# An encoder block on one core: the order of ScalarE and VectorE in its first stage, and of its last products

## The chip, the cores and the metric

One core of a Trainium2 chip runs the whole program once. The core has five engines with a queue of instructions each: TensorE (PE in the profile, PEld for its weight loads), VectorE (DVE), ScalarE (ACT), GpSimd (POOL) and SyncE (SP), which here only issues DMAs. An engine works through its queue in order; where an instruction needs another engine's result or a transfer, it waits on a semaphore, and everything behind it on its engine waits too. The metric is the device time of one execution in microseconds.

## What is computed

One layer of an encoder on 1024 tokens of 1024 channels, all in float32. Cut to what matters here:

```python
h = h + 0.5 * swiglu(rms_norm(h, ffn1_norm), w_gate, w_up, w_down)     # first stage
u = rms_norm(h, mix_norm); z = u @ w_in
h = h + (g_attn * attention(z) + g_ssm * s5(z)) @ w_out
h = h + 0.5 * swiglu(rms_norm(h, ffn2_norm), w_gate2, w_up2, w_down2)
h = h + (p @ w_ple) * sigmoid(rms_norm(h, ple_norm) @ w_ple_gate)
return rms_norm(h, final_norm)                                        # last stage

def rms_norm(x, g): return x * rsqrt(mean(x * x) + 1e-6) * g
def swiglu(x, wg, wu, wd): return (silu(x @ wg) * (x @ wu)) @ wd
```

The change touches how the first `rms_norm` and the first products of the first `swiglu` are started, and the end of the last `rms_norm`.

## The kernel before

Everything is held transposed: channels on the 128 partitions in eight tiles `h[j]`, tokens along the free axis in two halves, t=0 (columns 0 to 511) and t=1. A tile `h[j][t]` is 128x512. A matmul is done in three TensorE products (`mm3`, L190): each float32 operand is split into a rounded part and a remainder by `split` (L159): ScalarE writes the rounded part (`ph`, `xh`, `wh`; L160), VectorE subtracts it (`pl`, `xl`, `wl`; L161).

The first stage has three pieces of work.

- *The p products.* `p @ w_ple` is done at once, in the loop over n = 0..15 at the end of the quoted part: six products into a PSUM bank `pp`, a ScalarE copy out of it, and a DMA of 256 KB on GpSimd's queue. The table `hooks` says what else is written down ahead of the n-th step.
- *The norm of x.* `Norm.add` squares a tile (ScalarE) and adds it to `acc` (VectorE); `Norm.stat` sums over partitions with a matmul with `ones` into a bank `ms`, then `rstd` forms `rs`, with one ScalarE activation and three VectorE instructions. `Seven.norm` scales a tile in place (L337) and `Seven.put` splits it. `s7.nn[0]` is the norm of t=0 (`x0`), `s7.nn[1]` that of t=1 (`x1`). The four operands are named a11 and a12 (t=0, tiles 0-3 and 4-7) and a21 and a22 (t=1).
- *The FFN's first products.* `Ffn.run` first does eight C steps (11, 12, 22, 21; gate `g` and up `u` each), 24 products a step, with the first pair of column blocks of `w_gate` and `w_up`. Then come the A steps, which use seven products in place of eight and therefore need sums of operands (`sums`: s1, s3, s2, s4) and of weight blocks (`b_operand`); the operands of a step are written ahead of need by `prep`, and `need` and `prep` force the generator on.

Order: SyncE's loads stand in program order. Generators (`s7_first`, `sums`, `gen_all`) are moved on by `tick()`, once after each `mm3`, so that a `yield 14` is a distance in products. TensorE's instructions stand as written. VectorE's and ScalarE's are put in order by a scheduler, except between `order_cm.__enter__()` and `order_cm.__exit__()`, where they keep the order in which they are written among themselves; what is written outside may be put in between. In the kernel before this part ends with the p loop. The pairs of column blocks are numbered from 0 (the C steps); `begun` is called before the A steps of pair 2 (`("A", 2, 0, 0)`). GpSimd squares and sums four tiles of x1 in `x1_first`.

The last stage, `end`, finishes the last 256-column parts: `products(6, 2)` and `products(7, 2)` are 24 products each, `fin[1].stat` is the final norm's statistic of the columns 512 to 767, set by `after(7, ...)` seven `mm3` into them; `finish` scales two tiles at a time and stores them. There VectorE and ScalarE keep the written order too.

Of the kernel before, what the change touches and what calls it, by code (L numbers as in the profile page):

```python
# [20 lines left out]
NK = 8  # L21
# [20 lines left out]
def encoder_block(ctx, tc, I, out):  # L42
# [274 lines left out]
    class Seven:  # L317
# [3 lines left out]
        def __init__(self, h, gi, new_hi=None):  # L321
            self.h, self.gi = h, gi
            self.ops = {name: [] for name in ("a21",) + A7}
            self.last = []
            self.new_hi = new_hi or tw
            self.blk = [[at("hid", [P, HT], F32, "wblk") for _ in range(4)] for _ in range(2)]
            self.lo = [tx("wl") for _ in range(4)]
            self.nn = [Norm(h, t, thid("acc", dt=F32), thid("rs", dt=F32)) for t in range(2)]
            self.a21 = [(tx("xh"), tx("xl")) for _ in range(4)]
# [15 lines left out]
        def first(self, wait, then, every):  # L345
            yield wait
            self.nn[0].stat(self.nn[0].rs, self.nn[0].a0 is not self.nn[0].acc)
            yield then
            for name, j0 in (("a11", 0), ("a12", 4)):
                for k in range(4):  # L350
                    self.norm(j0 + k, 0)
                    self.put(name, self.h[j0 + k][0])
                    yield every

        def second(self, wait, every):
            yield wait
            self.nn[1].stat(self.nn[1].rs)
            yield 1
            for name, j0 in (("a21", 0), ("a22", 4)):
                for k in range(4):  # L360
                    self.norm(j0 + k, 1)
                    self.put(name, self.h[j0 + k][1])
                    yield 1

# [24 lines left out]
    class Ffn:  # L389
# [33 lines left out]
        def sums(self, every):  # L423
# [4 lines left out]
            def each(name, op, src):  # L428

                for k in range(4):  # L430
                    with behind_():
                        op(k)
                    S.put(name, src(k))
                    yield every
# [125 lines left out]
        def run_c(self, c, g):  # L560
            o = bank("gu"[g] + c)
            for half, (a, n) in enumerate((("a" + c[0] + "1", int(c[1]) - 1), ("a" + c[0] + "2", int(c[1]) + 1))):
                self.need(a)
                hi, lo = self.made["C", g, n]
                for k in range(4):
                    mm3(o, (hi[:, ksl(k)], lo[:, ksl(k)]), self.ops[a][k], half == 0 and k == 0, half == 1 and k == 3)
                    tick()
            with tc.high_priority(offset=PRI):
                self.evac_c(c, g, o)
# [385 lines left out]
    def begun():  # L955

        up_cm.__exit__(None, None, None)
        pools["gp"] = tc.tile_pool(name="gp", bufs=1)
# [4 lines left out]
    def p_split(x):  # L963
        split(*x[0], x[1])

    x0, x1 = s7.nn
    for k in range(2):
# [3 lines left out]

    def x1_first(j):
        if j == 0:
            x1.acc = x1.a0
            G.tensor_tensor(x1.acc, h[0][1], h[0][1], ALU.mult)
            return
        sq = tmp("sq")
        G.tensor_tensor(sq, h[j][1], h[j][1], ALU.mult)
        G.tensor_tensor(x1.acc, x1.acc, sq, ALU.add)

    def s7_first():
        yield from s7.first(14, 2, 2)
        for j in range(4, NK):
            x1.add(j)
        yield from chain(s7.second(6, 1), ffn.sums(2), gen_all())

# [5 lines left out]
             6: lambda: (p_split(pl_[0, 1]), p_split(pl_[1, 1])),  # L992
             9: lambda: x1_first(0), 10: lambda: x1_first(1), 11: lambda: x1_first(2), 12: lambda: x1_first(3),
             13: lambda: ffn.prep(("C", "11", 0))}
    start(s7_first())
    for n in range(2 * NK):
# [9 lines left out]
        nc.gpsimd.dma_start(pp_d[m, t], pp)  # L1006
    order_cm.__exit__(None, None, None)
    ffn.run()
# [826 lines left out]
    def end():  # L1835

        start(after(7, fin[1].stat))
        six = products(6, 2)
        drain()
        finish(1, (0,))  # L1840
        A.activation(six[2], six[0], AF.Sigmoid)
        added(*six)
        a, b, s, hm = products(7, 2)
        A.activation(s, a, AF.Sigmoid)
        fin[2].square(6, A)
        finish(1, (2,))
# [116 lines left out]
```

## Time and profile before

| | us |
|---|---|
| runs before (three) | 2104.4, 2106.75, 2111.21; median 2106.75 |
| profiled execution | 2106.68 |
| its span | 2104.9 |
| TensorE busy | 2040.9 (97%) |
| VectorE busy | 1495.0 (71%) |
| ScalarE busy | 1015.5 (48%) |
| GpSimd busy | 496.3 (24%) |
| mean granted clock of TensorE | 0.987 |

The profiled execution's time is the span and what lies around it (1.8 us). Busy time is a sum of instructions, and TensorE's are pipelined: a product lasts 0.39 us and the next starts 0.23 us later, so its 97% says that it nearly always has work, not that the work is done at its best rate. The page's slices show where it has none; the reader should look at the first and the last of them.

### The profile page before, as it was taken

What the parts mean: (1) busy time and instruction counts of PE and PEld (TensorE: products, weight loads), DVE (VectorE), ACT (ScalarE), POOL (GpSimd) and SP (SyncE); (2) the same over time, 40 slices, a digit from 0 to 9 for tenths busy, and PEclk for the clock granted to TensorE, in tenths of its full rate; (3) what the DMA queues carried; (4) which work ended last, traced back from release to release, by engine and by line L of the source; (5) the groups of instructions that cost most, each with busy time, mean ns of one, the idle gap of its engine ahead of it and who ended that gap; (6) DMA issues with size and microseconds to landing.
All of it is one profiled execution on the core that took longest, in us unless ns stands there. A gap on an engine that the chain in (4) does not pass through costs nothing.

```text
span 2104.9 us, 28181 instructions
## 1 busy us (share of the span) xinstructions
PE 2040.9 (97%) x9378; PEld 1687.5 (80%) x9378; DVE 1495.0 (71%) x2551; ACT 1015.5 (48%) x1908; POOL 496.3 (24%) x723
## 2 busy tenths in 40 slices
PE   5999999999999999999998999999999999999997
PEld 4788888888888887788887788788888888888886
DVE  5878787676696774788864668896656555796765
ACT  4533333334444443577766556553333333444554
POOL 2005565553000052888823002000000000000000
PEclk8899999999999999999999999999999999999999
DMA  6234344439443356787767688133332337443332
GB/s 221 95 118 132 124 135 128 139 119 327 153 153 113 120 143 172 235 233 227 242 192 234 205 299 200 61 100 136 101 124 81 120 101 281 134 146 99 107 98 88
DMA packets 216818, 328.15 MB, mean 156 GB/s; under 512 B 30688, under 2 KB 80480, under 8 KB 216672
## 3 DMA queue, kind: packets, MB, share of 16 engines
q1 hardware_dynamic: 174608, 266.53, 39.8%
q10 hardware_dynamic: 35664, 45.12, 6.5%
q0 software_dynamic: 6400, 14.70, 2.5%
q8 instruction: 74, 1.21, 0.2%
q14 instruction: 72, 0.59, 0.1%
HBM read 228.21 MB, written 98.04 MB: 155 GB/s over the span
## 4 chain that ended last, share of the span: by engine, by line
PE 85%; DVE 5%; DMA 5%; ACT 3%; issue 1%; SPq 1%; ACTq 0%; DVEq 0%; POOL 0%
PE dx L191 4%; PE dx L192 4%; PE dx L193 4%; PE ux L191 3%; PE gx L191 3%; PE gx L193 3%; PE ux L192 3%; PE ux L193 3%; PE gx L192 3%; PE dy L193 2%; PE dy L192 2%; PE dy L191 2%; PE uy L191 2%; PE gy L191 2%; PE uy L192 2%; PE gy L192 2%
## 5 line engine op out<-in xcount | busy, mean ns | idle before, releaser
L160 ACT CAST wh<-hbuf 128x512 fp32r<-128x512 f32 x280 | 173.7, 622 | 415.1 <-PE gx L192 90.4
L161 DVE TENSOR_TENSOR wl<-hbuf,wh 128x512 fp32r<-128x512 f32 x280 | 215.7, 772 | 123.7 <-ACT wh L160 121.5
L160 ACT CAST wh<-wblk 128x512 fp32r<-128x512 f32 x198 | 122.7, 622 | 200.1 <-PE dx L192 82.5
L161 DVE TENSOR_TENSOR wl<-wblk,wh 128x512 fp32r<-128x512 f32 x198 | 137.3, 696 | 64.1 <-ACT wh L160 56.6
L191 PE MATMUL dx<-ah,wh 128*128 128x512 f32 x416 | 163.5, 393 | 0.4 <-DVE hbuf L595 0.3
L193 PE MATMUL dx<-ah,wl 128*128 128x512 f32 x416 | 161.9, 389 | 0.0
L192 PE MATMUL dx<-al,wh 128*128 128x512 f32 x416 | 161.9, 389 | 0.0
L161 DVE TENSOR_TENSOR al<-araw,ah 128x512 fp32r<-128x512 f32 x154 | 106.4, 695 | 50.2 <-PE dx L192 21.2
L191 PE MATMUL ux<-xh,wh 128*128 128x512 f32 x320 | 125.0, 391 | 0.0
L191 PE MATMUL gx<-xh,wh 128*128 128x512 f32 x320 | 124.8, 390 | 0.0
L193 PE MATMUL gx<-xh,wl 128*128 128x512 f32 x320 | 124.5, 389 | 0.0
L192 PE MATMUL ux<-xl,wh 128*128 128x512 f32 x320 | 124.5, 389 | 0.0
L193 PE MATMUL ux<-xh,wl 128*128 128x512 f32 x320 | 124.5, 389 | 0.0
L192 PE MATMUL gx<-xl,wh 128*128 128x512 f32 x320 | 124.5, 389 | 0.0
L160 ACT CAST ah<-araw 128x512 fp32r<-128x512 f32 x154 | 95.0, 619 | 46.7 <-PE dx L192 14.2
L1122 POOL TENSOR_TENSOR sc<-X,rho 128x128 f32<-128x128 f32 x128 | 82.8, 647 | 64.5 <-ACT X L1105 54.6
L161 DVE TENSOR_TENSOR wl<-blk,wh 128x512 fp32r<-128x512 f32 x84 | 63.2, 755 | 48.7 <-ACT wh L160 44.6
L375 DVE TENSOR_TENSOR hbuf<-hbuf 128x512 f32<-128x512 f32 x120 | 91.6, 765 | 2.5 <-DMA hbuf<-in_wu 0.4
L191 PEld LDWEIGHTS dx<-ah,wh 128*128 128x128 f32 x416 | 78.1, 188 | 18.6 <-DVE hbuf L595 1.2
L192 PEld LDWEIGHTS dx<-al,wh 128*128 128x128 f32 x416 | 78.1, 188 | 16.8 <-issue 0.7
L193 PEld LDWEIGHTS dx<-ah,wl 128*128 128x128 f32 x416 | 78.1, 188 | 16.3
L191 PE MATMUL dy<-ah,wh 128*128 128x512 f32 x208 | 80.9, 389 | 0.0
(381 smaller groups left out, 5741.1 us busy)
## 6 DMA issues: line engine op xcount, KB each, us to landing
araw<-a_d SPq DMA_DIRECT2D x154, 256.0 KB, 2.6
a_d<-c SPq DMA_DIRECT2D x148, 256.0 KB, 2.1
wblk<-in_wd SPq DMA_DIRECT2D x88, 256.0 KB, 5.2
hbuf<-in_wg SPq DMA_DIRECT2D x40, 512.0 KB, 3.9
hbuf<-in_wu SPq DMA_DIRECT2D x40, 512.0 KB, 4.4
blk<-in_win ACTq DMA_DIRECT2D x48, 256.0 KB, 4.0
hbuf<-in_xT SPq DMA_DIRECT2D x32, 256.0 KB, 5.4
h_d<-hbuf ACTq DMA_DIRECT2D x32, 256.0 KB, 2.2
```

The costliest lines, as they stand in the source:

```text
L160: A.copy(hi, src)
L161: return eng.tensor_tensor(lo, src, hi.bitcast(F32), ALU.subtract)
L191: T.matmul(o, lhsT=wh, rhs=xh, start=first, stop=False, skip_group_check=more)
L192: T.matmul(o, lhsT=wh, rhs=xl, start=False, stop=False, skip_group_check=more)
L193: T.matmul(o, lhsT=wl, rhs=xh, start=False, stop=last, skip_group_check=more)
L375: V.tensor_tensor(b11, (b12, b22, None, None, b21)[i - 2], b11, ALU.subtract)
L1122: G.tensor_tensor(sc, both, rho4, ALU.mult)
```

## The change

It has six parts. (1) `order_cm.__exit__` moves from the end of the p loop into `begun`, so that VectorE and ScalarE keep the written order through the C steps and the A steps of pair 1, until pair 2. (2) `Seven.ahead` is 1 in the first FFN: the normalisation of tile j+1 is written ahead of the split of tile j, likewise in `sums`; it is 0 in the second FFN. (3) `x1_first` goes: all eight tiles of x1 are squared and added by ScalarE and VectorE, behind the splits of t=0; the second statistic stands 13 ticks behind them, not 6. (4) Weight splits of C11 for gate and up are both written at n = 12. The Silu of C11's gate, `evac_c("11", 0)`, is written ahead of the last of the eight `mm3` of C11's up step, behind the second statistic. (5) Ten 128x128 products of `ones` into a bank `idle` stand ahead of everything on TensorE. (6) At the end `fin[1].stat` stands two `mm3` later, `finish(1, (0,))` behind the last products, and tile 6's sigmoid and sums ahead of it.

```diff
@@ -322,7 +322,7 @@
             self.h, self.gi = h, gi
             self.ops = {name: [] for name in ("a21",) + A7}
             self.last = []
-            self.new_hi = new_hi or tw
+            self.new_hi, self.ahead = new_hi or tw, 1 if new_hi else 0
             self.blk = [[at("hid", [P, HT], F32, "wblk") for _ in range(4)] for _ in range(2)]
             self.lo = [tx("wl") for _ in range(4)]
             self.nn = [Norm(h, t, thid("acc", dt=F32), thid("rs", dt=F32)) for t in range(2)]
@@ -346,21 +346,24 @@
             yield wait
             self.nn[0].stat(self.nn[0].rs, self.nn[0].a0 is not self.nn[0].acc)
             yield then
-            for name, j0 in (("a11", 0), ("a12", 4)):
-                for k in range(4):
-                    self.norm(j0 + k, 0)
-                    self.put(name, self.h[j0 + k][0])
+            yield from self.operands(("a11", "a12"), 0, every)
+
+        def operands(self, names, t, every):
+
+            ahead = self.ahead
+            for j in range(NK + ahead):
+                if j < NK:
+                    self.norm(j, t)
+                if j >= ahead:
+                    i = j - ahead
+                    self.put(names[i // 4], self.h[i][t])
                     yield every
 
         def second(self, wait, every):
             yield wait
             self.nn[1].stat(self.nn[1].rs)
             yield 1
-            for name, j0 in (("a21", 0), ("a22", 4)):
-                for k in range(4):
-                    self.norm(j0 + k, 1)
-                    self.put(name, self.h[j0 + k][1])
-                    yield 1
+            yield from self.operands(("a21", "a22"), 1, 1)
 
     def taken_from(blk, i, src):
 
@@ -427,10 +430,12 @@
 
             def each(name, op, src):
 
-                for k in range(4):
-                    with behind_():
-                        op(k)
-                    S.put(name, src(k))
+                for k in range(4 + S.ahead):
+                    if k < 4:
+                        with behind_():
+                            op(k)
+                    if k >= S.ahead:
+                        S.put(name, src(k - S.ahead))
                     yield every
 
             def s1(k):
@@ -565,6 +570,11 @@
                 for k in range(4):
                     mm3(o, (hi[:, ksl(k)], lo[:, ksl(k)]), self.ops[a][k], half == 0 and k == 0, half == 1 and k == 3)
                     tick()
+                    if (c, g, half, k) == ("11", 1, 1, 2) and self.begun is not None:
+                        self.evac_c("11", 0, self.late)
+            if (c, g) == ("11", 0) and self.begun is not None:
+                self.late = o
+                return
             with tc.high_priority(offset=PRI):
                 self.evac_c(c, g, o)
 
@@ -954,6 +964,7 @@
 
     def begun():
 
+        order_cm.__exit__(None, None, None)
         up_cm.__exit__(None, None, None)
         pools["gp"] = tc.tile_pool(name="gp", bufs=1)
         pools["g"] = pools["gp"].__enter__()
@@ -963,26 +974,20 @@
     def p_split(x):
         split(*x[0], x[1])
 
+    idle = bank("idle")[:, 0:P]
+    for i in range(10):
+        T.matmul(idle, lhsT=ones, rhs=ones, start=True, stop=True)
     x0, x1 = s7.nn
     for k in range(2):
         p_split(pl_[k, 0])
         p_split(pr_[k])
     x0.add(0)
 
-    def x1_first(j):
-        if j == 0:
-            x1.acc = x1.a0
-            G.tensor_tensor(x1.acc, h[0][1], h[0][1], ALU.mult)
-            return
-        sq = tmp("sq")
-        G.tensor_tensor(sq, h[j][1], h[j][1], ALU.mult)
-        G.tensor_tensor(x1.acc, x1.acc, sq, ALU.add)
-
     def s7_first():
         yield from s7.first(14, 2, 2)
-        for j in range(4, NK):
+        for j in range(NK):
             x1.add(j)
-        yield from chain(s7.second(6, 1), ffn.sums(2), gen_all())
+        yield from chain(s7.second(13, 1), ffn.sums(2), gen_all())
 
     hooks = {1: lambda: (x0.add(1), x0.add(2)),
              2: lambda: (p_split(pr_[2]), x0.add(3)),
@@ -990,8 +995,7 @@
              4: lambda: (x0.add(5), x0.add(6)),
              5: lambda: x0.add(7),
              6: lambda: (p_split(pl_[0, 1]), p_split(pl_[1, 1])),
-             9: lambda: x1_first(0), 10: lambda: x1_first(1), 11: lambda: x1_first(2), 12: lambda: x1_first(3),
-             13: lambda: ffn.prep(("C", "11", 0))}
+             12: lambda: (ffn.prep(("C", "11", 0)), ffn.prep(("C", "11", 1)))}
     start(s7_first())
     for n in range(2 * NK):
         t, m = n // NK, n % NK
@@ -1004,7 +1008,6 @@
         pp = tmp("pp")
         A.copy(pp, o)
         nc.gpsimd.dma_start(pp_d[m, t], pp)
-    order_cm.__exit__(None, None, None)
     ffn.run()
     drain()
     pools["gp"].__exit__(None, None, None)
@@ -1834,15 +1837,15 @@
 
     def end():
 
-        start(after(7, fin[1].stat))
+        start(after(9, fin[1].stat))
         six = products(6, 2)
-        drain()
-        finish(1, (0,))
         A.activation(six[2], six[0], AF.Sigmoid)
         added(*six)
         a, b, s, hm = products(7, 2)
+        drain()
+        finish(1, (0,))
+        fin[2].square(6, A)
         A.activation(s, a, AF.Sigmoid)
-        fin[2].square(6, A)
         finish(1, (2,))
 
         A.activation(dummy, eps, AF.Abs_reciprocal_sqrt)
```

Where the rows moved. ScalarE, around the statistic of t=0 (`sq` are squares of x, `ph` casts of p's operands, `wh` casts of weight blocks, `pp` the copies, `rs` the statistic); before:

```order
L1005 COPY pp<-pp 128x512
L160 CAST ph<-pst 128x512
L230 ACTIVATE sq<-hbuf 128x512
L160 CAST wh<-wblk 128x512
L1005 COPY pp<-pp 128x512
L230 ACTIVATE sq<-hbuf 128x512 x2
L160 CAST wh<-wblk 128x512
L1005 COPY pp<-pp 128x512
L230 ACTIVATE sq<-hbuf 128x512
L1005 COPY pp<-pp 128x512
L160 CAST ph<-pst 128x512
```

After, on the same engine at the same place:

```order
L1009 COPY pp<-pp 128x512
L230 ACTIVATE sq<-hbuf 128x512 x2
L1009 COPY pp<-pp 128x512
L230 ACTIVATE sq<-hbuf 128x512
L1009 COPY pp<-pp 128x512
L160 CAST ph<-pst 128x512 x2
L212 ACT_TABLE_LOAD
L212 ACTIVATE rs<-ms,eps 128x512
L1009 COPY pp<-pp 128x512
```

Before, four `wh` casts stand among the squares and ahead of the table load for `rs` (two of them behind the rows shown); after, none does.

VectorE, the splits of t=0's operands (L337 normalises, `xl` is the split's remainder); before:

```order
L215 SCALAR_TENSOR_TENSOR rs<-rq,rs 128x512
L337 SCALAR_TENSOR_TENSOR hbuf<-hbuf,gains,rs 128x512
L161 TENSOR_TENSOR xl<-hbuf,xh 128x512
L337 SCALAR_TENSOR_TENSOR hbuf<-hbuf,gains,rs 128x512
L161 TENSOR_TENSOR xl<-hbuf,xh 128x512
L337 SCALAR_TENSOR_TENSOR hbuf<-hbuf,gains,rs 128x512
L161 TENSOR_TENSOR xl<-hbuf,xh 128x512
```

After, on the same engine at the same place:

```order
L215 SCALAR_TENSOR_TENSOR rs<-rq,rs 128x512
L337 SCALAR_TENSOR_TENSOR hbuf<-hbuf,gains,rs 128x512 x2
L161 TENSOR_TENSOR xl<-hbuf,xh 128x512
L337 SCALAR_TENSOR_TENSOR hbuf<-hbuf,gains,rs 128x512
L161 TENSOR_TENSOR xl<-hbuf,xh 128x512
L337 SCALAR_TENSOR_TENSOR hbuf<-hbuf,gains,rs 128x512
L161 TENSOR_TENSOR xl<-hbuf,xh 128x512
```

The normalisation of the next tile now stands ahead of the split that waits for ScalarE.

VectorE, from the last tiles of t=0 to the statistic of t=1 (`acc` are the sums of squares); before:

```order
L161 TENSOR_TENSOR xl<-hbuf,xh 128x512
L161 TENSOR_TENSOR wl<-wblk,wh 128x512 x2
L337 SCALAR_TENSOR_TENSOR hbuf<-hbuf,gains,rs 128x512
L161 TENSOR_TENSOR xl<-hbuf,xh 128x512
L337 SCALAR_TENSOR_TENSOR hbuf<-hbuf,gains,rs 128x512
L161 TENSOR_TENSOR xl<-hbuf,xh 128x512
L161 TENSOR_TENSOR wl<-wblk,wh 128x512 x2
L231 TENSOR_TENSOR acc<-acc,sq 128x512 x4
L213 TENSOR_TENSOR rq<-rs 128x512
```

After, on the same engine at the same place:

```order
L161 TENSOR_TENSOR wl<-wblk,wh 128x512 x4
L337 SCALAR_TENSOR_TENSOR hbuf<-hbuf,gains,rs 128x512
L161 TENSOR_TENSOR xl<-hbuf,xh 128x512
L337 SCALAR_TENSOR_TENSOR hbuf<-hbuf,gains,rs 128x512
L161 TENSOR_TENSOR xl<-hbuf,xh 128x512 x2
L231 TENSOR_TENSOR acc<-acc,sq 128x512 x7
L161 TENSOR_TENSOR wl<-wblk,wh 128x512 x4
L213 TENSOR_TENSOR rq<-rs 128x512
```

Four weight splits stand ahead of tile 6's normalisation, the four adds are seven, and four more weight splits stand between them and the statistic.

## The prediction

> **What bounds the kernel now.** I read the page first, for the span and the busy share by slice, then the waits of the first 75 us, then each engine's timeline there.
>
> ```profile
> span 2104.9 us, 28181 instructions
> PE   5999999999999999999998999999999999999997
> ...
> PE ms L258 <- DVE acc L231: 15.8, 2, 13.2
> ```
>
> The second line is TensorE's busy share in 40 slices of 52.6 us: full from the second slice to the last but one. So time can only be won in the first and the last slice, or be lost by starving TensorE between them. The wait (total, times, longest) names what holds the first: TensorE stands 13.2 us before the first `ms`, the matmul with `ones` that sums the squares of the columns 0 to 511 of x, the half t=0. The timelines of ScalarE, VectorE and TensorE show why (start, duration, engine, line; in brackets the idle time before, and what ended it):
>
> ```profile
> 12.98 0.64 ACT L230 ACTIVATE sq<-hbuf 128x512 f32<-128x512 f32 x1
> 26.02 0.62 ACT L160 CAST wh<-wblk 128x512 fp32r<-128x512 f32 x1 [12.40 <-DMA wblk<-in_wg]
> 28.07 0.61 ACT L160 CAST wh<-wblk 128x512 fp32r<-128x512 f32 x1
> 29.05 0.63 ACT L230 ACTIVATE sq<-hbuf 128x512 f32<-128x512 f32 x1
> 32.25 1.28 ACT L212 ACT_TABLE_LOAD   x1
> 33.55 0.69 ACT L212 ACTIVATE rs<-ms,eps 128x512 f32<-128x512 f32 x1
> ...
> 36.51 0.75 DVE L337 SCALAR_TENSOR_TENSOR hbuf<-hbuf,gains,rs 128x512 f32<-128x512 f32 x1
> 37.95 0.69 DVE L161 TENSOR_TENSOR xl<-hbuf,xh 128x512 fp32r<-128x512 f32 x1 [0.69 <-ACT xh L160]
> 40.88 2.07 DVE L337 SCALAR_TENSOR_TENSOR hbuf<-hbuf,gains,rs 128x512 f32<-128x512 f32 x1
> 59.23 0.69 DVE L161 TENSOR_TENSOR xl<-hbuf,xh 128x512 fp32r<-128x512 f32 x1 [0.68 <-ACT xh L160]
> 61.05 3.07 DVE L231 TENSOR_TENSOR acc<-acc,sq 128x512 f32<-128x512 f32 x4
> ...
> 64.18 2.07 PE L258 MATMUL ms<-acc,ones 128*128 128x512 f32 x2 [2.58 <-DVE acc L231]
> 67.98 0.39 PE L191 MATMUL u<-xh,wh 128*128 128x512 f32 x1
> 73.42 0.39 PE L191 MATMUL g<-xh,wh 128*128 128x512 f32 x1
> ```
>
> The reader is to see one chain. ScalarE stops at 13.5 (12.98 and 0.52 to the next start) and stands 12.4 us for a weight block, with three squares of x still undone behind it; statistics (`rs`) at 33.55; eight tiles normalised and split from 36.51 to 59.23 + 0.69 = 59.92; the last sums of x1 (the half t=1) to 64.12; the second `ms` at 64.18. From there TensorE runs on without a hole; its first C12 product (the third of the eight C steps) is at 73.42. I measure the front by that product.
>
> **The change part by part.** *1. The weight casts leave ScalarE's way.* In the new order the row behind the square of 12.98 is a copy, and up to the table load stand copy, two squares, copy, square, copy, two `ph` casts: eight instructions. From the cast at 28.07 to the square at 29.05, one copy between them, it is 0.98 us, 0.49 a row; with 0.51 for the eight they take 4.1, and the table load starts at 13.5 + 4.1 = 17.6, not 32.25; `rs`, 1.30 behind it, at 18.9 instead of 33.55. What could be late next:
>
> ```profile
> 5.92 2.50 SPq L874 DMA_DIRECT2D hbuf<-in_xT  x4
> hbuf<-in_xT SPq DMA_DIRECT2D x1, 256.0 KB, 5.5
> pst<-in_pT SPq DMA_DIRECT2D x1, 256.0 KB, 6.2
> ...
> 16.85 0.39 PE L193 MATMUL pp<-ph,pl 128*128 128x512 f32 x1
> ```
>
> The last of the eight x tiles of t=0 is issued near 8.0 and lands 5.5 later, at 13.5; its square is due at 15.5. The last `pst` tile, issued at 9.5, lands at 15.7; its cast is due at 17.1. The 42 `pp` products that stand before `ms` ended at 16.85 + 0.39 = 17.24; `ms` took 2.07 in the row at 64.18, at half clock, so about 1.0 here: 18.3, still ahead of 18.9. Nothing is late. **Minus 14.6.**
>
> *2. Ten idle products.* No row shows them. What they could change:
>
> ```profile
> 7.70 0.63 PE L192 MATMUL pp<-pl,ph 128*128 128x512 f32 x1
> 8.13 0.63 PE L193 MATMUL pp<-ph,pl 128*128 128x512 f32 x1
> 8.79 0.59 ACT L1005 COPY pp<-pp 128x512 f32<-128x512 f32 x1 [0.73 <-PE pp L193]
> ```
>
> The first `pp` products are spaced 0.43 us; later one takes 0.227 (24 from 67.98 to 73.42). ScalarE waits 0.73 us for them before its first copy, and then has no hole. If the idle products end that slow phase the wait goes: minus 0.7; if not, 0; if they still run when the first `ph` is there, plus 0.3. For their length the nearest row is the last-stage `ms` of 128x256 at half clock (below, about 1.0 us): half of that each, ten from 1.0, when `ones` is written, to 6.1 at worst. They keep TensorE busy right up to the first `pp` product, so I take **minus 0.7**.
>
> *3. One tile ahead, and no GpSimd sums.* Before, a tile's normalisation, cast and split ran one after the other (1.44 from 36.51 to 37.95, and 0.6 for the split: 2.05 us a tile), and some VectorE rows were stretched while GpSimd computed, as here:
>
> ```profile
> 71.24 0.68 DVE L161 TENSOR_TENSOR xl<-hbuf,xh 128x512 fp32r<-128x512 f32 x1
> 71.84 0.75 DVE L337 SCALAR_TENSOR_TENSOR hbuf<-hbuf,gains,rs 128x512 f32<-128x512 f32 x1
> 72.50 0.68 DVE L161 TENSOR_TENSOR xl<-hbuf,xh 128x512 fp32r<-128x512 f32 x1
> ...
> 41.33 1.06 POOL L978 TENSOR_TENSOR sq<-hbuf 128x512 f32<-128x512 f32 x1
> ```
>
> The 2.07 at 40.88 lies over the GpSimd square at 41.33; the same instruction takes 0.75 elsewhere. The rows at 71.24 to 72.50 show the pace with the normalisation ahead: 1.26 us a tile. So, with `rs` at 18.2 (after 2): first normalisation 2.96 later (as 33.55 to 36.51) at 21.2, first split 1.44 behind it, the fifth split four steps of 1.26 later, from 27.7 to 28.4. Then the order puts four weight splits in between, which follow ScalarE's four casts (from about 28.1, 0.52 each): to 31.3. Then the last three tiles, whose casts had to wait behind the weight casts: normalise, split, normalise, split, split: 0.66, 0.60, 0.66, 0.66 and 0.69 = 3.3: 34.6. That is 16.4 us after `rs` starts, against 59.92 - 33.55 = 26.4. **Minus 10.0.** TensorE's remaining 54 `pp` products end near 29.4, so it follows these splits closely.
>
> *4. The sums of x1, now eight squares and seven adds in one piece.* Before, four adds stood there, 3.07 us, so 0.77 each (each adds to the result of the one before). Now the first can run when ScalarE has done its last cast, a copy and two squares, near 35.5; seven adds end at 40.9, 6.3 us after the last split, against 64.18 - 59.92 = 4.26. **Plus 2.0.** The load that this needs, the eight x tiles of t=1, had landed by 26 before; even with eight 256 KB writes of `pp` moved ahead of them (about 0.7 us each at the 381 GB/s of that stage) that stays ahead of 34.
>
> *5. TensorE's products left behind the second `ms`.* Before, 30 of them: 73.42 - 64.18 = 9.24. Now nine. TensorE, done with the 39 others at about 38.6, waits 2.3 us and, as I read the clock, comes back at half speed, as at 64.18: `ms` and six products took 67.98 - 64.18 = 3.80; three more at 0.227 make 4.5. C12 starts at 45.4. **Minus 4.7.** Sum of the front: 73.4 - 45.4 = **28.0 us**.
>
> *6. What stands behind.* VectorE's second half is now later against TensorE: its first normalisation was at 69.25, 4.2 before C12; now it is at 40.9 + 2.1 + 2.96 = 46.0, 0.6 behind. That is a lag of 4.8 us on an engine that was full:
>
> ```profile
> 9.40:17.30 7.90, 7.84 (x35) 6.12 (x33) 3.97 (x6) 4.20 (x8) 1.85 (x3) 1.00 1.04 381
> 73.42:106.10 32.68, 32.68 (x146) 27.07 (x145) 31.93 (x53) 16.10 (x29) 0.04 (x1) 1.00 0.35 121
> 69.25 2.08 DVE L337 SCALAR_TENSOR_TENSOR hbuf<-hbuf,gains,rs 128x512 f32<-128x512 f32 x3
> 82.98 0.68 DVE L161 TENSOR_TENSOR xl<-hbuf,xh 128x512 fp32r<-128x512 f32 x1
> 104.37 0.69 DVE L161 TENSOR_TENSOR wl<-hbuf,wh 128x512 fp32r<-128x512 f32 x1
> 84.00 0.62 ACT L160 CAST wh<-hbuf 128x512 fp32r<-128x512 f32 x1 [0.89 <-DMA hbuf<-in_wg]
> hbuf<-in_wu SPq DMA_DIRECT2D x40, 512.0 KB, 4.4
> ```
>
> Its margins: the last split of this half (82.98 before) is first used 7 x 0.68 us into the step C22, which starts two steps of 5.44 (67.98 to 73.42 is one) behind C12: 15.7 us after C12 starts. Now eight normalisations of 0.66, eight splits and one gate product of 0.60 (10.7 us, and 0.6 of waiting for a table load) end 11.9 after it. 3.8 us remain. The first weight block that VectorE itself must form (split at 104.37) feeds a product that stands six C steps and four A steps of half their length behind the start of C12, at 73.42 + 32.6 + 10.9 = 117.0: 12 us early, now about 7. So the lag is hidden and costs 0; if the cover is gone it costs up to 4.8. Further back the order of all engines is as before up to the end.
>
> *7. The end.* There the statistics of the columns 512 to 767 (`fin[1]`) move six products back, and tile 6 of the last 256 columns is finished ahead of them:
>
> ```profile
> 2088.27 1.22 PE L258 MATMUL ms<-acc,ones 128*128 128x256 f32 x2 [3.60 <-DVE acc L231]
> 2091.21 0.35 PE L191 MATMUL pg<-xh,whh 128*128 128x256 f32 x1
> 2093.19 0.28 PE L192 MATMUL pg<-xl,whh 128*128 128x256 f32 x1
> 2093.63 0.38 ACT L1844 ACTIVATE ps<-pg 128x256 f32<-128x256 f32 x1 [1.85 <-PE pg L193]
> ```
>
> 27 products follow this `ms`; then ScalarE's last sigmoid at 2093.63, which waited for them, and all that follows hangs on it. Now 21 follow. The clock stays low until 2091.2 by time, not by count, so the six that go are fast ones, 0.12 each (2091.21 to 2093.19 is 17 of them). **Minus 0.7**; `rs` itself comes 0.2 later behind the earlier sigmoid, but VectorE then has tile 6 done, and waits for the sigmoid.
>
> Sum: 28.0 + 0.7 = 28.7. The profiled execution took 2106.68 (span 2104.9 and 1.8 around it), within 0.1 of the median 2106.75. 2106.7 - 28.7 = **2078.0 us**.
>
> **The rivals.** *Warm after the wait.* The window row of 61.6 to 64.2 has a granted clock of 0.93 over a 2.6 us wait, so it fell only in its last 0.4 us:
>
> ```profile
> 61.60:64.20 2.60, 0.02 (x1) 0.03 (x1) 2.21 (x4) 0.65 (x2) 0.54 (x1) 0.93 0.38 147
> ```
>
> A wait of 2.3 us is right at that edge. If the clock holds, `ms` (about 0.9 to the next product) and nine products of 0.227 take 2.9, not 4.5, and the time is 2076.4. The Trainium skill, TensorE: Matmul & The Clock Gate, Part 1, lets the clock go only after an idle window of about 3.4 us, so by it 2.3 us would be too short. The trace does not agree, since 2.6 us were enough here. I keep half clock as the likelier.
>
> *VectorE's lag shows.* If the 3.8 us are eaten, by casts that wait for weights (the bracket at 84.00 shows 0.89 of that), TensorE waits up to the lag of 4.8 and one landing of 4.4, and the time is up to 2087.
>
> *The wait only moves.* If ScalarE, in program order, meets another late load ahead of `rs` (the two `ph` casts: their `pst` tiles share engines that were busy 1.04 of the time in 9.4 to 17.3), the 12.4 us of the row at 26.02 come back and the time is 2090.4.
>
> *Slower.* In program order nothing may pass a cast that waits for its weights, and this holds up to pair 2 of the column blocks. Eight loads of 512 KB fall into it. If each cast is reached when its load is issued, ScalarE stands a landing of 4.4 us (the row of the DMA issues above) eight times, and TensorE with it: 2078 + 35 = 2113. It turns the sign from 28.7 / 8 = 3.6 us a load. Against it speaks the bracket at 84.00, 0.89, and that part 6 leaves 7 us between such a block and its product.
>
> **How the numbers follow.** The forecast has 0.50, the warm clock 0.20, the lag 0.14, the moved wait 0.11, slower 0.05. The floor is TensorE itself: 144 products of 0.227 and two `ms` of 0.9 end at 40.3 if they start at 5.8 (the copy at 8.79 less six products of 0.43 and 0.4 for the last to end); that is 5 us below 45.4: 2073. The range runs from there to 2087, just past the lag, and leaves out the last two, 0.16. A measurement of this kernel tells about 0.3% (6.3 us) from no change. Faster by more: the first four, 0.95; the slower case ends near that bound, so 0.04 slower by more and 0.01 within it.
>
> **What would show it.** No wait of ScalarE for a weight block ahead of `rs`, and `rs` near 18 to 19; the first five splits 1.26 apart; no GpSimd arithmetic before 75; second `ms` near 41 behind the last add; C12 near 45; no TensorE wait over 1 us from there to 130. A wait of C22 or of the first A steps for VectorE, or a `ms` later than 45, would prove the sum wrong.

## The result and the profile after

| | median us | range | runs |
|---|---|---|---|
| before | 2106.01 | 2104.4 to 2111.21 | 4 |
| after | 2075.01 | 2073.3 to 2078.53 | 4 |

The ratio is 0.9851, with a 95% interval of 0.9829 to 0.9872: 31 us less. The profiled execution took 2074.99. The same kernel, run again beside some of the experiments, took 2077.02 (2075.27 to 2078.28), against 2104.16 for the kernel before: 0.9868 (0.9853 to 0.9882), 27 us less. The forecast was 2078.0, 28.7 us less.

First the page's span and TensorE's busy slices:

```profile
span 2073.1 us, 28214 instructions
PE   9999999999999998999998999999999999999997
```

Then the one wait of the first 75 us over 1.2 us, from the view of TensorE's waits (total, times, longest):

```profile
PE ms L258 <- DVE acc L231: 1.9, 1, 1.9
```

The 13.2 us before the first `ms` are gone, and the first slice is full (4.6 us of it are the ten idle products). Then the timelines of ScalarE, VectorE and TensorE (start, duration, engine, line; in brackets the idle time before and what ended it):

```profile
8.14 0.59 ACT L1009 COPY pp<-pp 128x512 f32<-128x512 f32 x1 [0.17 <-PE pp L193]
18.18 0.69 ACT L212 ACTIVATE rs<-ms,eps 128x512 f32<-128x512 f32 x1
...
21.14 1.42 DVE L337 SCALAR_TENSOR_TENSOR hbuf<-hbuf,gains,rs 128x512 f32<-128x512 f32 x2
22.58 0.69 DVE L161 TENSOR_TENSOR xl<-hbuf,xh 128x512 fp32r<-128x512 f32 x1
23.85 0.68 DVE L161 TENSOR_TENSOR xl<-hbuf,xh 128x512 fp32r<-128x512 f32 x1
28.25 2.49 DVE L161 TENSOR_TENSOR wl<-wblk,wh 128x512 fp32r<-128x512 f32 x4
32.59 1.47 DVE L161 TENSOR_TENSOR xl<-hbuf,xh 128x512 fp32r<-128x512 f32 x2
34.89 5.48 DVE L231 TENSOR_TENSOR acc<-acc,sq 128x512 f32<-128x512 f32 x7 [0.84 <-ACT sq L230]
...
40.42 1.45 PE L258 MATMUL ms<-acc,ones 128*128 128x512 f32 x2 [1.91 <-DVE acc L231]
42.52 0.63 PE L193 MATMUL u<-xh,wl 128*128 128x512 f32 x1
42.94 0.63 PE L191 MATMUL u<-xh,wh 128*128 128x512 f32 x1
45.05 0.40 PE L191 MATMUL g<-xh,wh 128*128 128x512 f32 x1
```

`rs` starts at 18.18 instead of 33.55, the splits (`xl`) come 1.27 us apart instead of 2.05, the last of them ends at 32.59 + 1.47 = 34.06, the second `ms` stands at 40.42 and C12's first product at 45.05, where the forecast had 45.4. The products behind `ms` are 0.42 apart (42.52 to 42.94): half clock, as forecast (granted clock 0.50 from 41.4 to 44.5); more of that below.

To compare kernels I use a second mark, behind all that the change orders in the first stage: the first product `gz` of the A steps of pair 2 (the expectations call it the second pair). Before:

```profile
144.14 0.39 PE L191 MATMUL gz<-xh,wh 128*128 128x512 f32 x1
```

And after:

```profile
115.79 0.39 PE L191 MATMUL gz<-xh,wh 128*128 128x512 f32 x1
```

The front came out 28.35 us shorter at this mark, and the view of TensorE's waits lists none between C12 and it. From the mark to the end of the span it was 2104.9 - 144.14 = 1960.8 before and 2073.1 - 115.79 = 1957.3 after. A part of this 3.5 is the tail. VectorE's last two `rs` in its timeline, before:

```profile
2091.09 0.42 DVE L215 SCALAR_TENSOR_TENSOR rs<-rq,rs 128x256 f32<-128x256 f32 x1
2098.01 0.42 DVE L215 SCALAR_TENSOR_TENSOR rs<-rq,rs 128x256 f32<-128x256 f32 x1
```

And after:

```profile
2059.91 0.43 DVE L215 SCALAR_TENSOR_TENSOR rs<-rq,rs 128x256 f32<-128x256 f32 x1
2065.56 0.42 DVE L215 SCALAR_TENSOR_TENSOR rs<-rq,rs 128x256 f32<-128x256 f32 x1
```

They stand 6.92 us apart before and 5.65 after, 1.27 less. Not all of this is time won, since behind the second `rs` the span lasts 6.89 us before and 7.54 after. From the first `pg` product of 256 columns, which stands ahead of all that the change moved there (2076.24 before, 2045.13 after), to the end of the span it is 28.7 and 28.0 (28.2 in both later profiles of the changed kernel): the end brought 0.7 of the 3.5. The other 2.8 lie in a part in which the change moved nothing; what they are worth is shown at the end of the experiments.

### The profile page after: what moved, and what is told of

It reads as the page before. It is cut to its first block, busy times and chain, and to the rows that moved or that the text cites. A ratio compares the mean times of both kernels' runs of the same rounds, so it can differ in the third digit from the quotient of the medians.

```text
span 2073.1 us, 28214 instructions
## 1 busy us (share of the span) xinstructions
PE 2036.9 (98%) x9398; PEld 1687.8 (81%) x9398; DVE 1487.1 (72%) x2554; ACT 1016.8 (49%) x1912; POOL 488.2 (24%) x716
## 4 chain that ended last, share of the span: by engine, by line
PE 88%; DMA 5%; DVE 4%; ACT 2%; issue 1%; SPq 0%; ACTq 0%; DVEq 0%; POOL 0%
PE dx L191 4%; PE dx L192 4%; PE dx L193 4%; PE ux L191 4%; PE gx L191 4%; PE gx L193 4%; PE ux L193 4%; PE ux L192 4%; PE gx L192 3%; PE dy L192 2%; PE dy L191 2%; PE dy L193 2%; PE uy L191 2%; PE gy L191 2%; PE gy L193 2%; PE uy L193 2%
## 5 line engine op out<-in xcount | busy, mean ns | idle before, releaser
L161 DVE TENSOR_TENSOR al<-araw,ah 128x512 fp32r<-128x512 f32 x154 | 106.4, 695 | 50.2 <-PE dx L192 21.2
L192 PE MATMUL dy<-al,wh 128*128 128x512 f32 x208 | 80.9, 389 | 0.0
```

Source lines behind the costliest of these rows:

```text
L161: return eng.tensor_tensor(lo, src, hi.bitcast(F32), ALU.subtract)
L192: T.matmul(o, lhsT=wh, rhs=xl, start=False, stop=False, skip_group_check=more)
```

## The experiments

Each run is the changed kernel with one edit, but for the first kernel of experiment 3. "Mark" is the `gz` product above: 115.79 in the first profile of the changed kernel, and 115.8 and 114.8 in its two later ones.

**1. The length of the written order alone taken back.** Tile ahead, sums on VectorE, idle products and the end stay.

```diff
     def begun():
-        order_cm.__exit__(None, None, None)
...
         nc.gpsimd.dma_start(pp_d[m, t], pp)
+    order_cm.__exit__(None, None, None)
```

> The changed kernel with one part undone: the written order of VectorE and ScalarE ends with the p products again, as before. ScalarE then has four weight casts among its squares again, and the first of them waits for a load that landed at 26.0 before. My theory (this wait is half of the gain): rs near 33.4 instead of 18.2, then the same 22.2 us as in the changed kernel from rs to the second ms, so ms near 55.6 and the first C12 product near 60.2 instead of 45.05; time 2090. Rival (normalising ahead and the missing GpSimd sums carry the gain, and the wait only filled time that the front had anyway): C12 at 45 to 47, time 2075 to 2077.

It took 2092.16 us (2091.01 to 2093.12), 0.9937 of before (0.992 to 0.9954). TensorE's two `ms`:

```profile
30.43 2.05 PE L258 MATMUL ms<-acc,ones 128*128 128x512 f32 x2 [14.03 <-DVE acc L231]
55.66 1.12 PE L258 MATMUL ms<-acc,ones 128*128 128x512 f32 x2 [0.46 <-DVE acc L231]
```

The wait ahead of the first `ms` is back (14.0 us, 13.2 in the kernel before), `rs` stands at 33.42 and the second `ms` at 55.66, both 15.2 us later than in the changed kernel, as expected. C12 came at 58.70, not 60.2: the wait ahead of the second `ms` is only 0.46 us here, and the products behind it stay 0.23 apart. So at the mark, 129.4, 13.6 are left against the first profile of the changed kernel, and 14.6 against its second repetition, which had no half clock there either. Step 1 is shown: the weight casts among the squares cost what it said.

**2. The tile ahead alone taken away,** in the operands and in the FFN's sums.

```diff
-            self.new_hi, self.ahead = new_hi or tw, 1 if new_hi else 0
+            self.new_hi, self.ahead = new_hi or tw, 0
```

> The changed kernel with one part undone: each tile is normalised right ahead of its own split again. My theory (a tile then takes 2.05 us instead of 1.26, since the split waits for the cast and the cast for the normalisation): rs stays at 18.2, the last split of t=0 ends near 40.3 instead of 34.1, second ms near 46.6, C12 near 51.2; the second half's splits then end 17 us behind the start of C12, where TensorE wants them 15.7 behind it, so it may wait 1 to 2 us more in C22; time 2081 to 2083. Rival (VectorE's own work sets the pace, and the order within a tile is free): C12 at 45, time 2075.

It took 2100.75 us (2098.92 to 2106.22, ten runs), 0.9979 (0.9968 to 0.9989): nearly the whole gain was gone. The second `ms` came at 46.96, as expected. What I had not expected stands behind C12, in the view of TensorE's waits, 0 to 150 us (total, times, longest), the largest three:

```profile
PE gz L191 <- ACT wh L160: 4.9, 1, 4.9
PE ux L191 <- ACT wh L160: 3.0, 1, 3.0
PE gy L191 <- ACT wh L160: 2.6, 1, 2.6
```

And two splits of VectorE's timeline:

```profile
22.81 0.69 DVE L161 TENSOR_TENSOR xl<-hbuf,xh 128x512 fp32r<-128x512 f32 x1 [0.69 <-ACT xh L160]
24.86 0.69 DVE L161 TENSOR_TENSOR xl<-hbuf,xh 128x512 fp32r<-128x512 f32 x1 [0.69 <-ACT xh L160]
```

The two VectorE rows show the pace, 2.05 us a tile, with 0.69 us of it spent waiting for ScalarE's cast: in the written order nothing may fill that hole. The mark is 25.8 us late. 32 tiles are made that way ahead of it (16 operands, 16 sums), and 32 times 2.05 - 1.27 = 0.78 is 25.0. That sum leaves out two things that work against each other: the margins, which cover some of it, and the clock, which fell behind some of these waits, as in this window from 92 to 96 us (granted clock in the third column from the end):

```profile
92.00:96.00 4.00, 3.79 (x10) 2.99 (x11) 3.07 (x5) 1.29 (x3) 0.92 (x1) 0.57 0.38 123
```

That the two numbers come so close is therefore partly chance. But VectorE's and ScalarE's pace sets the whole front, not only the part up to C12 that I had priced.

**3. The written order alone, in the kernel before.** The mirror image of experiment 1.

```diff
     def begun():
+        order_cm.__exit__(None, None, None)
...
-    order_cm.__exit__(None, None, None)
     ffn.run()
```

> The kernel before with one part of the change alone: VectorE and ScalarE keep the written order until pair 2. My theory: rs at 18.9, then the 26.4 us to the last split as in the kernel before, so that one ends near 45.3; four adds to 48.9, second ms there, and the 30 products behind it as before: C12 near 58 instead of 73.4, time near 2091, 15 us under the kernel before. Rival (the parts need each other: without the tile ahead a strict order makes VectorE and ScalarE wait for each other and the later steps starve): C12 at 68 or later, or TensorE waits in C22 and the A steps, time 2100 or more.

It took 2109.14 us (2106.95 to 2116.37, ten runs), 1.002 of before (1.0008 to 1.0032): no gain at all, though its first `ms` came at 17.74 and its second at 49.93. Its two largest waits:

```profile
PE gz L191 <- ACT wh L160: 9.6, 1, 9.6
PE g L191 <- ACT wh L160: 8.1, 1, 8.1
```

These are 17.7 us of waiting for weight casts, against 6.4 in the kernel before (its `g` wait): most of the 13.2 before the first `ms` has only moved. The mark was at 147.2, 3.1 later than before. This kernel lacks the other parts of the change too, but experiment 2, where only the tile ahead is missing, has waits at the same products (`gz` 4.9, `gy` 2.6). Experiments 1 to 3 together: the order is worth about 14 us with the rest of the change, and nothing alone; without the tile ahead it moves the wait into the C and A steps.

**4. Where the tile ahead counts.** One kernel keeps it in the operands of x0 and x1 only, the other in the FFN's sums only.

```diff
 # operands only: in sums, each()
-                for k in range(4 + S.ahead):
+                for k in range(4):
...
 # sums only: in operands()
-            ahead = self.ahead
+            ahead = 0
```

> The tile ahead stays in the making of the operands from x0 and x1; the ffn's C22 and A steps split their tile in the step that makes it. Theory A (the 25.8 us that the kernel without a tile ahead lost came mostly from those later steps): next chunk's gate products at 45 as in the changed kernel, but behind it waits for wh and xh come back, 16 steps of about 0.75 us against margins of about 9 us: the second pair starts 3 to 15 us later than 115.8, time 2078 to 2090. Theory B (all from the operands): pair two at 115.8, time 2075.

> The other half: the operands of x0 and x1 are normalised and split tile by tile, the ffn's later steps keep the tile ahead. Theory A: second mean square at 46 to 47 as in the kernel without any tile ahead (5 to 6 us later), the next chunk's gate products at about 50, a22 late by 1 to 3 us, and no waits for wh and xh behind it: pair two 6 to 9 us later, time 2081 to 2084. Theory B (the two parts carry the loss together, and most of it stands here): pair two 15 us later or more, time above 2090.

Operands only: 2086.59 us (2083.38 to 2088.92), 0.991 (0.9886 to 0.9934), mark at 126.1, with 7.1 us of waits for `wh` in the A steps. Sums only: 2086.61 us (2083.16 to 2088.95), 0.991 (0.9886 to 0.9933), second `ms` at 47.33, mark at 125.8, a little more than expected. The parts lose 10.3 and 10.0 us of the 25.8: each is 16 tiles of 0.78, 12.5, less what the margins cover. Taken together they lose 5.5 more than the sum of the two. Margins that cover only once make up some 2 of it. The clock makes up about 3: up to the mark some 30 products stand 0.43 us apart with the tile ahead gone from both, where 10 and 8 do with it gone from one (5 in the changed kernel), and each costs 0.20.

**5. GpSimd.** First the old sums of four x1 tiles on GpSimd put back; then the changed kernel with four surplus squares on GpSimd that nothing reads.

```diff
 # first kernel
-        for j in range(NK):
+        for j in range(4, NK):
             x1.add(j)
...
+             9: lambda: x1_first(0), 10: lambda: x1_first(1), 11: lambda: x1_first(2),
+             12: lambda: (x1_first(3), ffn.prep(("C", "11", 0)), ffn.prep(("C", "11", 1)))}
 # second kernel, at the same four places
+    def spare(j):
+        G.tensor_tensor(x1.a0, h[j][1], h[j][1], ALU.mult)
```

> The changed kernel with one part undone: GpSimd squares and sums four tiles of x1 again, beside VectorE's splits. My theory (VectorE's rows are stretched while GpSimd computes; in the kernel before that was 5.8 us over seven GpSimd instructions, against 2.3 us for the three adds that VectorE is spared): last split of t=0 near 37 to 39 instead of 34.1, second ms near 41.5 to 43.5 instead of 40.4, C12 near 46 to 48; time 2076 to 2078. Rival (GpSimd's sums are free and their move to VectorE costs its three adds): ms at 38.1, C12 at 42.8, time 2072.7.

> The changed kernel with four surplus multiplies on GpSimd, one 128x512 square each of x1's first four tiles at the places where the old kernel squared them, into a buffer that nothing reads. Theory A (GpSimd's work stretches what VectorE does at the same time; in the kernel with GpSimd's sums seven such operations stretched four VectorE operations by about 7 us together): VectorE's operations beside them take 1.5 to 3 us in place of 0.7, about 1 us for each GpSimd operation, the second mean square stands at about 44 in place of 40.4, time about 2078. Theory B (GpSimd's sums cost 7 us because VectorE's sums wait for GpSimd's adds behind its DMA issues): no change here, second mean square at 40.4, time 2075.

With the sums: 2081.09 us (2079.71 to 2083.88), 0.9885 (0.9869 to 0.9901), second `ms` at 47.76, later than expected. With the surplus squares: 2079.3 us (2077.74 to 2080.96), 0.9878 (0.9862 to 0.9895), 2.3 over the changed kernel beside it, and second `ms` at 44.76, as theory A had it. GpSimd and VectorE in the second kernel:

```profile
24.03 1.05 POOL L987 TENSOR_TENSOR acc<-hbuf 128x512 f32<-128x512 f32 x1
26.16 1.05 POOL L987 TENSOR_TENSOR acc<-hbuf 128x512 f32<-128x512 f32 x1
...
23.91 1.73 DVE L161 TENSOR_TENSOR xl<-hbuf,xh 128x512 fp32r<-128x512 f32 x1
25.57 2.21 DVE L337 SCALAR_TENSOR_TENSOR hbuf<-hbuf,gains,rs 128x512 f32<-128x512 f32 x1
27.70 0.68 DVE L161 TENSOR_TENSOR xl<-hbuf,xh 128x512 fp32r<-128x512 f32 x1
```

The split at 23.91 takes 1.73 and the normalisation at 25.57 takes 2.21 beside a GpSimd square each; the next split, beside none, 0.68. Nothing waits for these squares, so it is their mere presence that costs. Four VectorE rows are stretched so, by 4.3 us together, which is what the second `ms` came later. It also goes the other way: the third square took 3.16 us, beside four weight splits that kept their 2.49. The Trainium skill (SBUF — State Buffer, Who interferes with whom) has this as a lock on a port that VectorE instructions with two inputs from SBUF share with GpSimd; these rows agree with it. With the real sums there was a second cost:

```profile
44.62 3.08 DVE L231 TENSOR_TENSOR acc<-acc,sq 128x512 f32<-128x512 f32 x4 [3.33 <-POOL acc L993]
```

VectorE's adds waited 3.3 us for GpSimd's, which stood in GpSimd's queue behind the DMA issues of `pp`, and these behind ScalarE's copies.

**6. The wait ahead of the second `ms` and the clock.** One kernel fills it with idle products; the other moves the statistic behind all 24 products of the up step, with both evictions of that chunk behind it; and the changed kernel itself was profiled twice more.

```diff
 # filled
+        def stat(self, r=None, summed=False, idle=0):
...
+                for _ in range(idle):
+                    T.matmul(m[:, 0:P], lhsT=ones, rhs=ones, start=True, stop=True)
...
 # late statistic
-        yield from chain(s7.second(13, 1), ffn.sums(2), gen_all())
+        yield from chain(s7.second(16, 1), ffn.sums(2), gen_all())
...
+                    if (c, g, half, k) == ("12", 0, 0, 1) and self.begun is not None:
+                        for g_, late in enumerate(self.late):
+                            self.evac_c("11", g_, late)
```

> Nine idle 128x128 products stand ahead of the second mean square, where TensorE waits 1.9 us for VectorE's last add. Theory A (the idle stretch before it lowers the clock): with TensorE busy, the 24 products' rest behind the mean square keep 0.21 us or so each in place of 0.43, the next chunk's gate products start about 43.4 in place of 45.05, the time is about 2073.4. Theory B (the clock falls for another reason, for instance the load since the start): products still 0.43 apart from 41 to 44, the gate products at 45.0 and the time 2075.

> The second mean square moves behind all 24 products of the chunk at hand; both of that chunk's evictions move into the next chunk's first half. Theory A (the statistic's place is all that still costs): in the changed kernel VectorE's last add of x1 ends about 40.4 and the 24 products end at 40.55, so TensorE no longer waits 1.9 us ahead of the second mean square, the clock has no hole to fall behind, the statistic starts at 40.5 and the next chunk's gate products at about 41.4 in place of 45.05; the operands made from x1 are not later than in the changed kernel, so TensorE must still find them: last split of a22 near 56.6 against a need near 57.1. Time about 2071.5. Theory B (the lag shows): the operand tiles come too late for TensorE's earlier need, waits of 2 to 4 us appear in the products that read a21 and a22, the second pair of chunks starts at 115.8 as before, and the time stays at 2075.

> The changed kernel itself, once more, for the clock behind the second mean square. Theory A (each 1.9 us wait lowers the clock): products behind it 0.43 us apart from 41 to 44 as in its first profile, next chunk's gate products at 45.05. Theory B (the clock falls in some executions only, as the kernel with the tile ahead in its operands alone had the same 1.9 us wait and its products stayed 0.23 apart): gate products at 43.5 in one at least of the two profiles, second pair at 114.3 in place of 115.8. The rest of the program should differ from the first profile by no more than 2 or 3 us.

> As again_1: gate products behind the second mean square at 45.05 (theory A) or, in this or the other profile, at 43.5 (theory B).

TensorE in the second repetition:

```profile
40.32 1.13 PE L258 MATMUL ms<-acc,ones 128*128 128x512 f32 x2 [1.90 <-DVE acc L231]
41.51 0.39 PE L192 MATMUL u<-xl,wh 128*128 128x512 f32 x1
41.74 0.39 PE L193 MATMUL u<-xh,wl 128*128 128x512 f32 x1
43.36 0.39 PE L191 MATMUL g<-xh,wh 128*128 128x512 f32 x1
```

The same wait, 1.90 us, and this time the products behind it stay 0.23 apart, and C12 starts at 43.36. In the first repetition it was so too (wait 1.93, C12 at 43.96). So half clock behind this wait is a matter of the single execution: of five profiles with a wait of 1.90 to 1.96 us there (the changed kernel three times, operands only, and experiment 7) it came once. Behind 2.14 us (sums only) it did not come, behind 2.24 us (GpSimd's sums), 2.58 us (the kernel before) and 3.18 us (experiment 3) it did. The Trainium skill (TensorE: Matmul & The Clock Gate, Part 1) says that the gate watches a free-running window, which fits a drop that comes by chance, and that it takes an idle window of about 3.4 us, which does not: 1.91 us were enough.

Filled: 2070.67 us (2069.22 to 2076.52), 0.9842 (0.9812 to 0.9872); C12 at 43.68, but the mark at 115.36. Late statistic: 2076.86 us (2074.86 to 2077.81), 0.9864 (0.9842 to 0.9885); no wait, C12 at 41.03, mark at 114.6. Of the 4.0 us by which C12 came earlier, 1.2 were left at the mark. Another 0.4 was never won: the second `ms` ends under C12's first product, and the next one starts 0.63 behind it. The other 2.4 went into the A steps of pair 1, where two waits appeared, 1.6 of the 2.4, with slower starts around them:

```profile
PE uy L191 <- ACT wh L160: 0.8, 1, 0.8
PE gx L191 <- DVE c L505: 0.8, 1, 0.8
```

The repetitions lost 1.1 and 0.7 us, and the filled kernel 1.0, in the same A steps. So behind C12 TensorE now runs as early as VectorE and ScalarE deliver; whoever wants more of the front must make their work less. The lowest median of all is that of the filled kernel, but its interval overlaps that of the changed kernel, and its mark lies between those of the changed kernel's profiles. That it is faster is not shown.

**7. The two small parts, taken back together:** no idle products at the start, and the old order of the end.

```diff
-    for i in range(10):
-        T.matmul(idle, lhsT=ones, rhs=ones, start=True, stop=True)
...
-        start(after(9, fin[1].stat))
+        start(after(7, fin[1].stat))
```

> The changed kernel without its ten idle products and with the old order of the last steps. Theory A (each is worth what the prediction gave it): first copy of pp waits about 0.7 us for TensorE, rs at about 18.9 in place of 18.2, second mean square about 0.7 later, and the tail from the last statistic to the end of the span about 0.7 us longer; time about 2076.4. Theory B (the idle products matter more, since the clock then rises about 4 us later: first products at half speed until about 10): rs at 20 or later, time 2078. Theory C (nothing): 2075.

It took 2081.52 us (2079.47 to 2085.82), 0.9892 (0.9876 to 0.9908), 4.5 over the changed kernel beside it. TensorE's and ScalarE's first rows, and the tail:

```profile
7.24 0.63 PE L193 MATMUL pp<-ph,pl 128*128 128x512 f32 x1
7.67 0.63 PE L191 MATMUL pp<-ph 128*128 128x512 f32 x1
...
9.19 0.59 ACT L1006 COPY pp<-pp 128x512 f32<-128x512 f32 x1 [1.04 <-PE pp L193]
11.37 0.59 ACT L1006 COPY pp<-pp 128x512 f32<-128x512 f32 x1 [0.55 <-PE pp L193]
19.88 0.69 ACT L212 ACTIVATE rs<-ms,eps 128x512 f32<-128x512 f32 x1
...
2064.13 0.42 DVE L215 SCALAR_TENSOR_TENSOR rs<-rq,rs 128x256 f32<-128x256 f32 x1
2071.13 0.42 DVE L215 SCALAR_TENSOR_TENSOR rs<-rq,rs 128x256 f32<-128x256 f32 x1
```

Without the idle products the first `pp` products stay 0.43 apart, here until 10.7; ScalarE waits for them twice, 1.04 and 0.55 us, and `rs` comes 1.70 us later, more than twice the 0.7 forecast (theory B had 20 for it). How long this slow phase lasts differs: it ended at about 9.0 in the kernel before and at 10.4 in experiment 3, neither of which has idle products. The mark, at 116.67, is 0.9 to 1.9 later than in the three profiles of the changed kernel. At the end the last two `rs` are 7.00 apart again, not 5.65, and from the first `pg` product of 256 columns to the end of the span it is 29.2, 1.2 more than in the changed kernel. So the two parts are worth about 1.7 and 1.2 us, 2.9 together; the other 1.6 of the 4.5 is not placed by these rows.

**The part that nothing touched.** From the mark to the end of the span the profiles of experiments 4 to 7 and of the changed kernel have 1953.5 (filled) to 1962.0 us (experiment 7, 1.2 of it the tail). The window from 700 to 800 us shows one source (window, length, busy time of PE, PEld, DVE, ACT and POOL, granted clock, DMA share, GB/s); the changed kernel's:

```profile
700.00:800.00 100.00, 95.85 (x475) 80.45 (x474) 66.44 (x98) 43.76 (x87) 32.97 (x26) 0.98 0.57 163
```

And the filled kernel's:

```profile
700.00:800.00 100.00, 96.33 (x486) 80.94 (x485) 66.32 (x98) 44.80 (x88) 31.06 (x24) 1.00 0.59 167
```

TensorE has short waits there in both, but the clock fell to 0.98 in one and stayed at 1.00 in the other. So a difference of two or three us in the span can come from here; this is why the mark was read beside the times. It is also why the filled kernel, at 2070.67, lies below the 2073 that the prediction called the floor, though its C12 came at 43.68 and not at 40.3: the floor took the rest of the program as fixed.

## Why the prediction was right, and where it was not

The time, the sum of the front and the order of events held; the size of one term and one margin did not.

1. *Weight casts out of ScalarE's way, 14.6 us.* Experiment 1 has `rs` 15.2 us later and the mark 13.6 to 14.6. The eight rows up to the table load were forecast at 4.1 behind the end of the square, 4.6 from its start; in experiment 7 they took 4.7 (from the square at 13.89 to the load at 18.59). Its `rs` stands at 19.88 and not at the 18.9 of this step because all of it begins 0.9 later, behind the slower first products.
2. *Idle products, 0.7.* 1.7 by experiment 7. The step took the wait for the first copy from one profile, in which the slow phase ended at about 9.0; where it lasted to 10.7, the first copy waited longer and the second waited too. With idle products it ended at about 7, and `rs` came at 18.18 against 18.2. That these agree to 0.02 is luck: nine other profiles with idle products and the written order have 18.08 to 18.78 there.
3. *One tile ahead and no GpSimd sums, 10.0.* The rows came within 0.6 us of the forecast (first normalisation 21.14 against 21.2, last split's end 34.06 against 34.6). But the step priced the tile ahead up to the second `ms` only. Its value in the whole front is 25.8 us, since the FFN's sums need it as much. The sum did not suffer, as both ends of the change were counted with the tile ahead in place; the price of the change without it would have been wrong by some 18 us, as the expectation for experiment 2 was.
4. *Sums of x1, plus 2.0.* Second `ms` at 40.42 against 40.9.
5. *Nine products behind it, wait 2.3, half clock.* Wait 1.91, and half clock in the profiled execution, C12 at 45.05 against 45.4. The repetitions show that the rival "warm after the wait" is the commoner course at this place, so it was luck that the first profiled execution took the course of the forecast. The choice is worth less than its 1.6 us: the mark moved by 0.0 and 1.0, since VectorE and ScalarE then set the pace. The place of the statistic was never put back by itself, so this term is read from rows and not from a run of its own.
6. *VectorE's lag is hidden.* No wait is listed from C12 to the mark in the first profile. But the margin for the first weight blocks, 7 us, was far too large. VectorE's split for the first `gy` step and the product that reads it, in that profile:

```profile
87.55 0.69 DVE L161 TENSOR_TENSOR wl<-hbuf,wh 128x512 fp32r<-128x512 f32 x1 [0.69 <-ACT wh L160]
89.04 0.39 PE L193 MATMUL gy<-xh,wl 128*128 128x512 f32 x1
```

The split ends at 88.24, 0.8 us ahead of its use. The step took the 12 us of the kernel before, where this split stood at 104.37, and subtracted only the lag of 4.8; but in the written order the block is also formed later, behind VectorE's last work on the C steps: 42.5 us behind the start of C12 and not 31.0. That the lag cost nothing was luck as well: with C12 1.1 and 1.7 us earlier, in the repetitions, 1.1 and 0.7 us were lost here.

7. *The end, 0.7.* 0.7 against the kernel before, 1.2 by experiment 7, from the first `pg` product of 256 columns to the end of the span. The size agrees partly by chance: the step took fast products away behind a slow phase that ends, but in the first profile after the change the products behind this `ms` are fast first (0.12 apart from 2057.61 to 2058.32) and then slow (0.21 from 2058.47 on).

The rival "the wait only moves" had the wrong place (casts of `pst` ahead of `rs`), but its mechanism is real: it is what the written order does without the tile ahead, as experiments 2 and 3 show. The rival "slower" had the wrong cause, since from C12 to the mark ScalarE waited for no weight load, in the changed kernel as in experiment 3; but the order alone did make the kernel no faster.

## What to carry to other kernels

Keeping a written order on two engines that hand tiles to each other paid here only because the order itself left each of them something to do while the other worked: one tile of distance turned 2.05 us a tile into 1.27 and decided over nearly the whole gain. When a change bundles an order with a distance, price the pace through all the steps that use it, not only up to the first wait that goes. And when a leading part becomes shorter, take a mark behind it: the time of the whole moved by several us for reasons that lay elsewhere.

## What the runs showed of the hardware that was not expected

- The granted clock fell behind a wait of 1.91 us in one profile of five, and only about 0.7 us after work had resumed at 40.42 (the windows of the trace have 1.00 up to 40.9, 0.69 from 40.9 to 41.4, then 0.50), for 3.4 us.
- A GpSimd square of 1.05 us, whose result nobody reads, stretched the VectorE instruction beside it by 1.05 (0.68 to 1.73) and 1.46 us (0.75 to 2.21), its own length or more.
